# Shifting all SBUF tiles behind one small tile by 224 bytes in a Strassen QKV projection

## The chip, the cores and the metric

The kernel runs on one core of a Trainium2 chip. The metric is the device time of one execution in microseconds, as a median over executions; the span of a profile is about 2 us shorter than the time of the same execution. An execution counts as slow when it took over 1.5% more than the fastest of the same kernel, and as fast otherwise; of a program that ran once the state is unknown.

## The reference

```python
batch, seq, hidden = 16, 512, 768          # x: 16x512x768 float32, w_qkv: 768x2304 float32
qkv = np.matmul(x, w_qkv)
q, k, v = qkv[..., :hidden], qkv[..., hidden:2*hidden], qkv[..., 2*hidden:]
return np.stack([q, k, v], axis=0).astype(np.float32)
```

So it is one matrix product of 8192 rows by 768 by 2304, with the columns stored in three parts.

## The kernel before

The 2304 columns are two groups of 1024 (q=0 and q=1 in the code, called a and b here when they are used in a turn; a5 is product 5 of group a) and a remainder of 256. For each group and each 256 rows of x, a Strassen scheme makes the 2x2 block product from seven block products. Products 1 and 2 are in bf16, 3 to 7 in f32 (the type float32r). Each is three matmuls of 128x128 weights and 512 moving columns. A matmul has two operands: the weights, for which the trace shows a load of its own before each matmul, and the moving operand. The weights here are tiles of x (xb in bf16, or the sums s in f32), and the moving operands are tiles of w (b1 in bf16, t and b22 in f32).

```python
w_pool = ctx.enter_context(tc.tile_pool(name="w", bufs=1))
tq_pool = ctx.enter_context(tc.tile_pool(name="tq", bufs=2))
...                                   # bt, o, st, or, xin, xf pools
xb_pool = ctx.enter_context(tc.tile_pool(name="xb", bufs=4))
s_pool = ctx.enter_context(tc.tile_pool(name="s", bufs=2))
...
w_rem = w_pool.tile([P, KT, REM], bf16, name="w_rem")
b1 = [w_pool.tile([P, KT, CB], bf16, name=f"b1_{q}") for q in range(2)]
b22 = [w_pool.tile([P, KH, CB], f32r, name=f"b22_{q}") for q in range(2)]   # of both groups, product 3
t_0 = w_pool.tile([P, 4, KH, CB], f32r, name="t_0")          # moving tiles of group a
...
zero = w_pool.tile([P, CB], bf16, name="zero")
tiny = w_pool.tile([P, 1], fp32, name="tiny")                # takes 32 bytes
eye = w_pool.tile([P, P], bf16, name="eye")                  # 256 bytes, last tile of the pool w
...
t_1 = [tq_pool.tile([P, 2, KH, CB], f32r, name=f"t_1{n}", tag="tq") for n in range(2)]  # of group b
```

The next cut is condensed.

```python
def product(u, n, ps, start):
    t1, t2, t3, t4 = ts[u.q]
    if n <= 2:
        lhs, rhs = ...                # bf16: xb and b1
    else:
        k, t = {3: (4, b22[u.q][:]), 4: (0, t4), 5: (1, t1), 6: (2, t2), 7: (3, t3)}[n]
        lhs = [sr[u.p][:, k, j, :] for j in range(KH)]       # from an s tile
        rhs = [t[:, j, :] for j in range(KH)]
    for j in range(KH):
        nc.tensor.matmul(ps[:], lhs[j], rhs[j], ...)

def two(a, b, early):                 # one turn: 256 rows, both groups
    do(a, 1); do(b, 1); early()
    do(a, 2); do(a, 6); do(b, 2); do(b, 6)
    do(a, 5); do(a, 7); do(b, 5); do(b, 7)
    do(a, 4); rem(a.p); do(b, 4)      # rem: 12 bf16 matmuls of 256 columns
    do(a, 3); store_quad(a); do(b, 3); store_quad(b)
```

Pools lie one behind the other in SBUF. tiny and eye are the only tiles here whose size per partition is not a multiple of 512 bytes. So the size of eye, the last tile of w, decides at which byte, modulo 512, everything behind it starts.

Of the kernel before, what the change touches and what calls it, by code (L numbers as in the profile page):

```python
# [10 lines left out]
def kernel(  # L11
# [20 lines left out]
    nc = tc.nc  # L32
    P = 128
# [15 lines left out]
    bf16 = mybir.dt.bfloat16  # L49
# [9 lines left out]
    w_pool = ctx.enter_context(tc.tile_pool(name="w", bufs=1))  # L59
# [77 lines left out]
    def copy_halves(dst, src, two):  # L137

        nc.vector.tensor_copy(out=dst[0], in_=src[0])  # L139
        if two:  # L140
            nc.scalar.activation(dst[1], src[1], ident)  # L141
        else:
            nc.vector.tensor_copy(out=dst[1], in_=src[1])
# [10 lines left out]
    def turn_rows(p, two=True):  # L154
        c = xc.pop(p)
        xb[p] = xb_pool.tile([P, KT, 2 * P], bf16, name="xb")
        for r in range(2):
            cols = c[:, r, :].rearrange("m (p j) -> m j p", j=KT)
            ps = ps_pool.tile([P, KT, P], bf16, name="ps")
            for j in range(KT):  # L160
                nc.tensor.transpose(ps[:, j, :], cols[:, j, :], eye[:])  # L161
            ks = (slice(0, KH), slice(KH, KT))
            copy_halves(
                [xb[p][:, n, r * P:(r + 1) * P] for n in ks], [ps[:, n, :] for n in ks], two
            )
# [175 lines left out]
    load_rows(0)  # L341
    tiny = w_pool.tile([P, 1], fp32, name="tiny")
    nc.scalar.activation(tiny[:], zero[:, :1], ident)
    eye = w_pool.tile([P, P], bf16, name="eye")
    make_identity(nc, eye)
    load_rows(1)
    load_blocks(0, 0, 1)
# [64 lines left out]
    busy(11)  # L412
    cast_rows(0)
    turn_rows(0)
    busy(4)
    cast_rows(1)
    cast_k(0)
    cast_k(1)
    turn_rows(1)
    for j in range(2, KT):  # L420
        cast_k(j)
# [7 lines left out]
    rem(1)  # L429
    cast_rows(2, False)  # L430
    turn_rows(2, False)
    block(0, 0, b1[0], halves((4, 5)), nothing)
    for h in range(2):
# [63 lines left out]
```

## Time and profile before

| | before |
|---|---|
| median time | 367.14 us (366.95 to 367.59, 3 runs) |
| span of the profile | 364.8 us |
| TensorE busy | 358.0 us, 98% |
| granted TensorE clock, mean | 0.997 |
| period of one turn (42 matmuls of 512 columns, 12 of 256) | 10.873 us |

To read it: PE stands for TensorE's matmuls, PEld for its weight loads, DVE for VectorE, ACT for ScalarE, POOL for GpSimd. In a group row the number after x is the count, then come busy time in us, mean duration of one in ns, and the idle time of the engine just before. Matmul durations overlap, so a duration of 390 ns does not mean that one matmul takes 390 ns of the engine. What counts is the distance from one start to the next. Each position within a turn has nearly always the same distance (mostly within 2 ns), so a mean over turns resolves tenths of a nanosecond. The lines are in the prediction.

### The profile page before, as it was taken

What the parts mean: (1) busy time and instruction counts of PE and PEld (TensorE: products, weight loads), DVE (VectorE), ACT (ScalarE), POOL (GpSimd) and SP (SyncE); (2) the same over time, 40 slices, a digit from 0 to 9 for tenths busy, and PEclk for the clock granted to TensorE, in tenths of its full rate; (3) what the DMA queues carried; (4) which work ended last, traced back from release to release, by engine and by line L of the source; (5) the groups of instructions that cost most, each with busy time, mean ns of one, the idle gap of its engine ahead of it and who ended that gap; (6) DMA issues with size and microseconds to landing.
All of it is one profiled execution on the core that took longest, in us unless ns stands there. A gap on an engine that the chain in (4) does not pass through costs nothing.

```text
span 364.8 us, 5274 instructions
## 1 busy us (share of the span) xinstructions
PE 358.0 (98%) x1797; PEld 243.8 (67%) x1797; DVE 225.8 (62%) x239; ACT 182.4 (50%) x304; POOL 173.7 (48%) x180
## 2 busy tenths in 40 slices
PE   7999999999999999999999999999999999999995
PEld 3544576666776666776666777676777676777663
DVE  3589746765557665557666556666556766556732
ACT  4557554454454454554455544545545444445442
POOL 0000961655665445665444665444665544566410
PEclk9999999999999999999999999999999999999998
DMA  7999979988899899999888899888899989899767
GB/s 297 382 375 336 347 245 335 327 284 293 273 313 311 264 285 296 277 301 321 278 274 289 281 300 318 284 271 284 288 297 310 296 258 292 291 286 316 261 251 267
DMA packets 80617, 108.08 MB, mean 296 GB/s; under 512 B 4816, under 2 KB 60368, under 8 KB 80592
## 3 DMA queue, kind: packets, MB, share of 16 engines
q1 hardware_dynamic: 65184, 96.35, 80.8%
q10 hardware_dynamic: 15408, 11.41, 9.9%
q8 instruction: 14, 0.23, 0.3%
q14 instruction: 11, 0.09, 0.1%
HBM read 32.24 MB, written 75.50 MB: 295 GB/s over the span
## 4 chain that ended last, share of the span: by engine, by line
PE 97%; DMA 1%; ACT 1%; DVE 0%; issue 0%
PE ps L206 76%; PE ps L256 12%; PE ps L381 9%; DMA xin<-in_x_dram 1%; PE ps L161 1%; ACT xc L141 0%; ACT xb L141 0%; DVE xb L139 0%; ACT orem L311 0%
## 5 line engine op out<-in xcount | busy, mean ns | idle before, releaser
L206 PE MATMUL ps<-t,s 128*128 128x512 f32 x696 | 188.0, 412 | 0.0
L206 PEld LDWEIGHTS ps<-t,s 128*128 128x128 f32 x696 | 128.7, 188 | 30.9
L169 POOL CAST xb<-xf 128x1536 bf16<-128x1536 f32 x29 | 43.9, 1514 | 171.6 <-DVE xf L124 160.1
L124 DVE STREAM_TRANSPOSE xf<-xin 128x1536 f32<-128x1536 f32 x29 | 86.8, 2991 | 6.8 <-DMA xin<-in_x_dram 3.9
L206 PE MATMUL ps<-b,xb 128*128 128x512 bf16 x348 | 85.2, 381 | 0.0
L240 DVE TENSOR_TENSOR o<-o,ps 128x512 f32<-128x512 f32 x58 | 39.9, 688 | 59.3 <-PE ps L206 59.2
L234 DVE TENSOR_TENSOR o<-o,ps 128x512 f32<-128x512 f32 x58 | 39.8, 687 | 54.1 <-ACT o L233 54.1
L206 PEld LDWEIGHTS <-xb 128*128 128x128 bf16 x348 | 29.4, 98 | 42.8 <-issue 14.7
L233 ACT ACTIVATE o<-ps 128x512 f32<-128x512 f32 x58 | 34.8, 600 | 45.2 <-PE ps L206 45.2
L220 ACT ACTIVATE o<-ps 128x512 f32<-128x512 f32 x58 | 34.7, 599 | 43.3 <-DVE o L240 34.6
L227 ACT ACTIVATE o<-ps 128x512 f32<-128x512 f32 x58 | 34.8, 600 | 41.9 <-PE ps L206 41.9
L256 PE MATMUL ps<-w_rem,xb 128*128 128x256 bf16 x384 | 47.5, 273 | 0.0
L206 PE MATMUL ps<-b,s 128*128 128x512 f32 x174 | 44.9, 393 | 0.0
L256 PEld LDWEIGHTS <-xb 128*128 128x128 bf16 x384 | 35.0, 98 | 12.4 <-issue 8.1
L224 DVE TENSOR_TENSOR o<-o,ps 128x512 f32<-128x512 f32 x58 | 36.5, 669 | 2.3 <-ACT o L220 1.3
L206 PEld LDWEIGHTS ps<-b,s 128*128 128x128 f32 x174 | 32.7, 188 | 7.7
L237 ACT ACTIVATE o<-ps 128x512 f32<-128x512 f32 x58 | 34.7, 598 | 4.5 <-ACT orem L311 0.4
L178 POOL TENSOR_TENSOR s<-s,xf 128x384 fp32r<-128x384 f32 x29 | 30.1, 1038 | 2.3
L177 POOL TENSOR_TENSOR s<-xf 128x384 fp32r<-128x384 f32 x29 | 30.9, 1066 | 0.0
L266 ACT ACTIVATE orem<-ps 128x512 f32<-128x512 f32 x31 | 18.6, 599 | 23.5 <-PE ps L256 23.5
L181 POOL TENSOR_TENSOR s<-xf,s 128x384 fp32r<-128x384 f32 x29 | 29.5, 1019 | 0.0
L179 POOL TENSOR_TENSOR s<-xf 128x384 fp32r<-128x384 f32 x29 | 29.2, 1006 | 0.0
(36 smaller groups left out, 128.1 us busy)
## 6 DMA issues: line engine op xcount, KB each, us to landing
out_dram<-o SPq DMA_DIRECT2D x62, 768.0 KB, 5.2
out_dram<-o SPq DMA_DIRECT2D x65, 256.0 KB, 4.8
xin<-in_x_dram SPq DMA_DIRECT2D x62, 192.0 KB, 6.8
xin<-in_x_dram ACTq DMA_DIRECT2D x54, 192.0 KB, 5.6
out_dram<-orem SPq DMA_DIRECT2D x31, 256.0 KB, 2.3
st<-in_w_qkv_dram SPq DMA_DIRECT2D x6, 768.0 KB, 14.1
xin<-in_x_dram SPq DMA_DIRECT2D x3, 768.0 KB, 5.8
st<-in_w_qkv_dram SPq DMA_DIRECT2D x6, 256.0 KB, 6.2
```

The costliest lines, as they stand in the source:

```text
L124: nc.vector.transpose(t[:].rearrange("p j (g b) -> p g j b", b=G), xin.pop(p)[:].rearrange("p g (a j) -> p g j a", a=G),)
L169: nc.gpsimd.tensor_copy(out=xb[p][:], in_=xf[p][:])
L206: nc.tensor.matmul(ps[:], lhs[j], rhs[j], start=(start and j == 0), stop=(j == KH - 1), skip_group_check=True,)
L220: nc.scalar.activation(c11, u.x[:], ident)
L224: nc.vector.tensor_tensor(c11, c11, u.z[:], op=add)
L227: nc.scalar.activation(c12, u.x[:], ident)
L233: nc.scalar.activation(c22, u.x[:], ident)
L234: nc.vector.tensor_tensor(c22, c22, u.y[:], op=add)
L237: nc.scalar.activation(c21, u.x[:], ident)
L240: nc.vector.tensor_tensor(c12, c12, u.y[:], op=add)
L256: nc.tensor.matmul(ps, xb[p][:, j, r * P:(r + 1) * P], w_rem[:, j, :], start=(j == 0), stop=(j == KT - 1), skip_group_check=True,)
L381: nc.tensor.matmul(ps[n][:], xb[p][:, j, r * P:(r + 1) * P], w[:, j, :], start=(j == 0), stop=(j == KT - 1), skip_group_check=True,)
```

## The change

The intent is to have all operands of all products start at one offset modulo 512 bytes. eye keeps its 128 columns, but its tile is 240 columns wide, so 480 bytes are taken in place of 256.

```diff
-                nc.tensor.transpose(ps[:, j, :], cols[:, j, :], eye[:])
+                nc.tensor.transpose(ps[:, j, :], cols[:, j, :], eye)
...
-    eye = w_pool.tile([P, P], bf16, name="eye")
+
+    eye = w_pool.tile([P, 240], bf16, name="eye")[:, :P]
```

By the addresses that the allocator gives, w_rem, b1, b22 and t_0 lie at 128 modulo 512 in both kernels; t_1, xb, s and the rest lie at 416 before and at 128 after. b22 of both groups lies in w, so product 3 of b, too, had its operands at different offsets before.

## The prediction

> **What bounds the kernel now.** I read the page first: the busy row, the chain that ended last and the costliest groups. Then the chain in order of time, then short windows of the timeline, and last the start times of the individual matmul records of the trace.
>
> ```profile
> PE 358.0 (98%) x1797; PEld 243.8 (67%) x1797; DVE 225.8 (62%) x239; ACT 182.4 (50%) x304; POOL 173.7 (48%) x180
> ...
> PE 97%; DMA 1%; ACT 1%; DVE 0%; issue 0%
> ...
> L206 PE MATMUL ps<-t,s 128*128 128x512 f32 x696 | 188.0, 412 | 0.0
> L206 PEld LDWEIGHTS ps<-t,s 128*128 128x128 f32 x696 | 128.7, 188 | 30.9
> ...
> L206 PE MATMUL ps<-b,xb 128*128 128x512 bf16 x348 | 85.2, 381 | 0.0
> L206 PEld LDWEIGHTS <-xb 128*128 128x128 bf16 x348 | 29.4, 98 | 42.8 <-issue 14.7
> ...
> L206 PE MATMUL ps<-b,s 128*128 128x512 f32 x174 | 44.9, 393 | 0.0
> ```
>
> TensorE carries 97% of the chain, and its matmuls have 0.0 us of idle before them. No other engine is above 62%. So only the rate at which TensorE takes its matmuls sets the time, and a wait anywhere else is slack. The chain in order of time shows how regular this is:
>
> ```profile
> 161.10 1.33 PE ps L256 x12
> 162.43 9.55 PE ps L206 x42
> 171.97 1.33 PE ps L256 x12
> ```
>
> One turn of the loop (256 rows of x, both column groups) is 12 short and 42 long matmuls. Its period, from the start records, is 10.873 us, the same within 8 ns in all turns. There are 29 turns (the last in another order), so 315 of the 365 us are such turns.
>
> The matmul durations of the page overlap, so I used the distance from one start to the next. Means over 28 turns, in ns, the three matmuls of a product in order; a and b are column groups q=0 and q=1, the number is the Strassen product:
>
> a6 419, 229, 238; b6 417, 229, 233 (the first of each includes what the record before it gave up: 28+419 is 216+231); a5 234, 230, 235; a7 231, 229, 235; b5 231, 226.65, 226.65; b7 226.65 three times; a4 234, 235, 232; b4 314, 231, 236; a3 235, 231, 231; b3 229, 235, 232. Every bf16 product stands at 215.8, the 256-column ones at 109.
>
> So matmuls of one shape and type differ by up to 9 ns, each position always alike. Two windows of the timeline, a5 with a7 and then most of b5 with b7, show it without the records:
>
> ```profile
> 157.49 1.56 PE L206 MATMUL ps<-t,s 128*128 128x512 f32 x6
> ...
> 159.11 1.30 PE L206 MATMUL ps<-t,s 128*128 128x512 f32 x5
> ```
>
> Six overlapping records last five distances and one duration (394 ns in that window): (1.56-0.394)/5 = 233 ns. Five last four distances and one of 389 ns: (1.30-0.389)/4 = 228 ns. Same clock (1.00 in this stretch).
>
> What differs is the place of the operands. From the pool sizes of the kernel before, the pool w ends 288 bytes (tiny padded to 32, eye 256) past a multiple of 512 from its start. Thus w_rem, b1, b22, t_0 share one offset modulo 512 (128 by the allocator's addresses), and tq (t_1), xb, s and all later tiles share another (416). Each block of s, t, b1 and xb used here is a multiple of 512 or half of it. While an f32 matmul of a streams t_0 or b22 (128), the weights of the next are loaded from s (416); while one of b5 or b7 streams t_1 (416), weights come from s (416). Only this latter case reaches 226.65.
>
> **What the Trainium skill says.** (1) "TensorE: Matmul & The Clock Gate", section "Back-to-back issue gap": N/2.4 + 2.5 ns, thus 215.8 for 512 columns and 109.2 for 256. The trace agrees to 0.1 ns for bf16. So bf16 products have nothing to gain. (2) The same page, "Weight-path perf modes": fast weight load is on for 128 weights unless the type is FP32. The trace agrees in kind: loads of 98 ns in bf16, 188 in f32. In the fastest f32 stream a load starts 3 ns after the matmul before it, lasts 187.7, and the next matmul starts 35.6 ns after its end: 226.3. I take this as the floor for f32: weight loads, not columns. (3) "SBUF — State Buffer", "Who interferes with whom": TensorE has two independent read ports, one for the moving operand, one for weights, and PE never waits on anyone. The trace does not sit well with this: in the slow positions the lag from load end to matmul start is 40 to 45 ns instead of 35.6, though nothing but the operands' places differs. Neither page mentions a period of 512 bytes. (4) "DMA: Bandwidth & Descriptors", "How a descriptor splits into AXI transactions": starts at multiples of 256 B cost least. After the change the tiles lie at 128 modulo 256, before at 160, so neither has that; no run here shows an effect.
>
> **The change part by part.** It adds no instruction and removes none. eye takes 480 bytes in place of 256, so everything behind the pool w moves up by 224: 416 becomes 640, which is 128 modulo 512. All operands of all products then have one offset. The total grows by 224 bytes per partition and still fits. The identity keeps its place and is read by 36 transposes in the first 18 us only.
>
> What each position gains, taking b5/b7 as the model of an aligned stream (226.65), one settling step of 231 where a run of f32 has just begun (as b5 shows on its first), and nothing at positions where q=1 was aligned already:
> - a6: the first 419 to 417 as in b6 (2.5), the last before bf16 238 to 232 as in a4 and b3 (6.4): 9
> - a5: 3 + 3.3 + 8.4 = 15; a7: 4.2 + 2.5 + 8.4 = 15; b5: 4
> - a4: 7.6 + 8.4 = 16, its last (before bf16) stays
> - a3: 4 + 4.2 + 4.2 = 12; b3: 2.5 + 8.4 = 11, its last stays
> - b6, b7, b4: 0
>
> Sum 82 ns per turn, all on the path since TensorE has no idle. Times 29 turns: 2.4 us. The bf16 start (to 43.6 us, 216 ns per matmul) and the tail of 4.4 us stay. 367.14 - 2.4 = 364.7 us, a change of -0.65%.
>
> The uncertain step is settling. b6 and b4 are aligned now and yet run at 229, 233 and 231, 236: right after a switch from bf16, alignment did not help within three matmuls. If in the new kernel those also settle at once, the gain rises by about 31 ns (b6 9, b4 13, a5 and a3 4 each) to 113 ns: 3.3 us, 363.8. If the stream takes several more matmuls to settle after each switch, perhaps half the gain remains: 1.2 us, 365.9.
>
> **The rivals.** First: not equality but the absolute place of the moving operand counts (416 good, 128 bad). The evidence for it is equally b5 and b7, for they are the only t_1 streams long enough. Then b5 and b7 fall to the level of a5 and a7 (695 in place of 684 and 680, some 26 to 30 ns per turn): +0.9 us, 368.0. Against it: a mechanism of two reads meeting depends on their difference, and b6/b4, also at 416, are not fast. I give it one in six. Second: the two offsets do not matter, and phase alone (how far the load lags after a switch) makes the pattern; then nothing moves, 367.1. One in eight. Against it: b7 to a4 goes from 226.65 to 234 at the very change of moving operand, with no switch between. Third: the gain uncovers another bound. TensorE would need 0.8% less per turn, while from 43.6 to 356.8 us DVE is busy 194 of 313 us, ACT 155, POOL 165, and the DMA share is 0.90 at 291 GB/s (358 in the stretch before, so it can go higher). None becomes the bound. Fourth: DMA gains from the new places. In the steady turns it is hidden; only the first load (4.3 us of the chain) and the last stores could show, a tenth of a microsecond or two at most.
>
> **Range and chances.** Most of the weight lies between 363.8 and 365.9 around 364.7, with a quarter to a third for the first two rivals at 367 to 368. The range 363.4 to 366.9 should hold it 8 times in 10. To be faster by over 2% (under 359.8) a turn would have to lose 253 ns, but with every f32 matmul at the load floor of 226.65 it loses at most about 130. Slower by over 2% would need 250 ns more per turn, where the worst position now is 11 ns above the floor. So within 2% is nearly sure.
>
> **What would show it right or wrong.** Right: the pieces of 42 matmuls in the chain fall from 9.55 to about 9.47 us while those of 12 stay at 1.33; the x6 window of a5 and a7 falls from 1.56 to about 1.52; the group t,s falls from a mean of 412 to about 409.5, b,s from 393 to about 389; bf16 groups stay at 381 and weight loads at 188. The first rival: the windows of a and b become alike at the slower level. The second: the positions keep their numbers. Wrong in size: the positions right after a bf16 product show how long settling takes. The prediction fails outright if TensorE gets idle time, or if bf16 distances leave 216.

## The result

The changed kernel takes 365.01 us (364.97 to 365.77, 6 runs) against 367.04 us (366.92 to 367.59, 6 runs). The ratio is 0.9946, with a 95% interval of 0.9933 to 0.9958. A ratio here is the mean time of one kernel's fast runs over that of the other's in the same rounds, so it is not quite the ratio of the medians quoted. A change clear of noise, and within the 2% that count as the same.

The page of the changed kernel, in the same parts as before (busy row, groups):

```profile
PE 354.3 (98%) x1765; PEld 244.0 (67%) x1797; DVE 224.2 (62%) x239; ACT 182.2 (50%) x304; POOL 173.8 (48%) x180
...
L206 PE MATMUL ps<-t,s 128*128 128x512 f32 x696 | 186.5, 410 | 0.0
L206 PEld LDWEIGHTS ps<-t,s 128*128 128x128 f32 x696 | 128.8, 188 | 29.7
...
L206 PE MATMUL ps<-b,s 128*128 128x512 f32 x174 | 44.5, 391 | 0.0
```

The reader should see three things. The f32 matmuls are 2 ns shorter on the mean (412 to 410 and 393 to 391). The weight loads have their old 188 ns. And this trace holds 1765 matmuls for 1797 weight loads: 32 matmul records are missing, so its busy time is not to be compared (all 696 + 174 f32 matmuls are there). The same kernel was therefore profiled again (the run after_again below), and that trace is complete. Its chain in order of time (start in us, length in us, what), around one turn:

```profile
160.62 1.33 PE ps L256 x12
161.94 9.48 PE ps L206 x42
```

The 12 short matmuls are as before, and the 42 long ones went from 9.55 to 9.48 us. Its timeline in the two windows that the prediction used, a5 with a7 and then most of b5 with b7:

```profile
157.05 1.52 PE L206 MATMUL ps<-t,s 128*128 128x512 f32 x6
...
158.64 1.30 PE L206 MATMUL ps<-t,s 128*128 128x512 f32 x5
```

The window of group a fell from 1.56 to 1.52 us, and that of b stayed at 1.30. With a duration of 389 ns in the first window the distance is (1.52-0.389)/5 = 226 ns: group a has come to the level of b. The period of a turn fell from 10.873 to 10.807 us in both traces of the changed kernel. That is 66 ns, and over 29 turns 1.9 of the 2.0 us between the medians.

### The profile page after: what moved, and what is told of

It is laid out like the page before. It is cut to its first block, busy times and chain, and to the rows that moved or that the text cites. A ratio compares the mean times of both kernels' runs of the same rounds, so it can differ in the third digit from the quotient of the medians.

```text
span 362.8 us, 5242 instructions
## 1 busy us (share of the span) xinstructions
PE 354.3 (98%) x1765; PEld 244.0 (67%) x1797; DVE 224.2 (62%) x239; ACT 182.2 (50%) x304; POOL 173.8 (48%) x180
## 4 chain that ended last, share of the span: by engine, by line
PE 96%; ACT 1%; issue 1%; ACTq 0%; DVE 0%
PE ps L206 75%; PE ps L256 11%; PE ps L382 9%; PE ps L362 1%; PE ps L161 0%; ACT o L237 0%; ACTq L297 0%; ACT xb L141 0%; ACT orem L311 0%; DVE xb L139 0%; ACT xc L141 0%; ACTq L313 0%; DVE zero L340 0%; ACTq L311 0%
## 5 line engine op out<-in xcount | busy, mean ns | idle before, releaser
L169 POOL CAST xb<-xf 128x1536 bf16<-128x1536 f32 x29 | 46.4, 1600 | 169.5 <-DVE xf L124 167.5
L206 PE MATMUL ps<-b,xb 128*128 128x512 bf16 x320 | 79.0, 380 | 1.9
L233 ACT ACTIVATE o<-ps 128x512 f32<-128x512 f32 x58 | 34.7, 598 | 44.1 <-PE ps L206 44.1
L177 POOL TENSOR_TENSOR s<-xf 128x384 fp32r<-128x384 f32 x29 | 29.3, 1010 | 0.0
L179 POOL TENSOR_TENSOR s<-xf 128x384 fp32r<-128x384 f32 x29 | 29.1, 1002 | 0.0
```

The costliest lines, as they stand in the source:

```text
L169: nc.gpsimd.tensor_copy(out=xb[p][:], in_=xf[p][:])
L206: nc.tensor.matmul(ps[:], lhs[j], rhs[j], start=(start and j == 0), stop=(j == KH - 1), skip_group_check=True,)
L233: nc.scalar.activation(c22, u.x[:], ident)
```

## The experiments

The twelve runs were made in three sets; each set was timed beside the kernel before on one chip. "Difference" means the start of s less the start of the moving tile. In the kernel before it is 288 for group a and 0 for b, in the changed kernel 0 for both. Product 3 of b goes with group a in this, since its moving tile b22 lies beside t_0. The diffs are against the changed kernel unless they say otherwise. A padding tile that is never used costs no instruction.

### all_416: all operands together at another place

```diff
+    lead = w_pool.tile([P, 144], bf16, name="lead")      # 288 bytes, ahead of w_rem
     w_rem = w_pool.tile([P, KT, REM], bf16, name="w_rem")
```

> The changed kernel with 288 unused bytes ahead of all tiles: all operands at 416 modulo 512 in place of 128. Theory (equality): pattern and time of the changed kernel, settled f32 matmuls at 226.65, a turn of 10.807 us, 365.0 us, ratio about 0.9946. Rival (s at 128 is what is good, 416 is bad for it): a5, a7, a4 and b5, b7 slow, 230 to 235, time of the kernel before or 1 us above.

Measured: 365.66 us (365.0 to 365.75), ratio 0.9957 (0.9943 to 0.9972), turn 10.807 us. Every position of a turn has the distance it has in the changed kernel, within 0.5 ns. Its chain around one turn has the pieces of the changed kernel:

```profile
160.96 1.33 PE ps L257 x12
162.28 9.48 PE ps L207 x42
```

So the place itself does not count, neither that of s nor that of the moving tile. The executions fall on two levels, 365.0 and about 365.7; in the profiled one (365.62) the first long matmuls of the turns stand in the chain at 45.48 us, in the changed kernel's (364.97) at 44.84, so what differs lies ahead of the turns. The changed kernel too had one execution at 365.77, so the new place is not needed for it; why it came oftener here (three of four) is open.

### half: a difference of 256 for group a

```diff
-    eye = w_pool.tile([P, 240], bf16, name="eye")[:, :P]
+    eye = w_pool.tile([P, 368], bf16, name="eye")[:, :P]
```

> Padding of eye such that s and t_1 lie at 384 and t_0, b22 at 128: difference 256 in column group 0, 0 in group 1. Theory (period of 512): group 0 stays slow, b5 and b7 stay at 226.65, time within 1 us of the kernel before (366 to 368). Rival (the period is 256 or a divisor of it): group 0 as fast as in the changed kernel, ratio 0.9946.

Measured: 365.67 us (365.03 to 365.79), ratio 0.9958 (0.9943 to 0.9973), turn 10.807 us. Its timeline in the window of a5 with a7:

```profile
156.82 1.52 PE L206 MATMUL ps<-t,s 128*128 128x512 f32 x6
```

It reads as in the changed kernel, though s lies 256 bytes off t_0. My expectation was wrong and its rival right: the rule needs no 512, and 256 (or a divisor of it) is enough.

### near: differences of 32 bytes

```diff
+    gap_pool = ctx.enter_context(tc.tile_pool(name="gap", bufs=1))   # between xb and s
     s_pool = ctx.enter_context(tc.tile_pool(name="s", bufs=2))
...
+    gap = gap_pool.tile([P, 16], bf16, name="gap")
...
-    eye = w_pool.tile([P, 240], bf16, name="eye")[:, :P]
+    eye = w_pool.tile([P, 208], bf16, name="eye")[:, :P]
```

> s lies 32 bytes behind t_1 (difference +32, group 1) and 32 bytes ahead of t_0 and b22 (difference -32, group 0), modulo 512. Theory as told (exact equality): both groups slow, 229 to 236, turn of 10.88 us or more, ratio 1.000 to 1.004. Rival (only a coarse distance counts, 32 bytes are next to nothing): both fast, ratio 0.9946. If one sign is fast and the other slow, the order of the two reads counts and not equality.

Measured: 369.11 us (369.02 to 369.39), ratio 1.0058 (1.0041 to 1.0074), turn 10.940 us. Its timeline in the windows of a5 with a7 and of b5 with b7:

```profile
158.37 1.56 PE L208 MATMUL ps<-t,s 128*128 128x512 f32 x6
...
160.00 1.33 PE L208 MATMUL ps<-t,s 128*128 128x512 f32 x5
```

Now b is slow as well: (1.33-0.396)/4 = 234 ns with the 396 ns of that window. So 32 bytes, ahead or behind, are enough to lose the pace. (With a period of 256, the 288 of the kernel before are 32 as well.) The turn is 67 ns above the kernel before (a slow, b fast) and 133 ns above the changed kernel (both fast). Of the 67 ns, 47 stand in b6, b5, b7 and b4, which lost their equal offset; the other 20 stand in products that had unequal offsets in both kernels (a6 and b3 above all), so it seems to count somewhat in which way two operands are apart. The kernel before thus had a third to a half of what equal offsets are worth without the change.

### mid: differences of 128 and 64 bytes

```diff
+    gap = gap_pool.tile([P, 32], bf16, name="gap")       # 64 bytes, between xb and s
...
-    eye = w_pool.tile([P, 240], bf16, name="eye")[:, :P]
+    eye = w_pool.tile([P, 272], bf16, name="eye")[:, :P]
```

> s stands 128 bytes past t_0 and b22 (group 0) and 64 bytes past t_1 (group 1). The run half showed 256 to be as good as 0. If the period is 256: both groups slow, 229 to 236, turn about 10.94 us as in near, some 369 us. If it is 128: group 0 fast, group 1 slow. If it is 64 (near excludes 32): both fast, 365.0 us.

Measured: 368.43 us in its one execution (state unknown, granted clock 0.997), turn 10.927 us. Its timeline in the windows of a5 with a7 and of b5 with b7:

```profile
158.00 1.55 PE L208 MATMUL ps<-t,s 128*128 128x512 f32 x6
...
159.62 1.33 PE L208 MATMUL ps<-t,s 128*128 128x512 f32 x5
```

In group a (difference 128) a5 and a7 have distances of 228 to 233 ns, in b (64) b5 and b7 have 231 to 239. Neither reaches 226.65. A period of 128, or of any divisor of it, would have made 128 as good as 0. So the period is 256.

### s16: 16 and 48 bytes

```diff
-        s = s_pool.tile([P, 5, KH, P], f32r, name="s")
+        s = s_pool.tile([P, 5 * KH * P + 8], f32r, name="s")
+        s = s[:, 4:4 + 5 * KH * P].rearrange("p (a j m) -> p a j m", a=5, j=KH)
```

> The changed kernel with the contents of s moved by 16 bytes within tiles that are 32 bytes longer, so that s stands 16 bytes past t_0, t_1 and b22 in every second turn and 48 bytes past them in the others. Theory (only equality modulo 256 counts): no position settles at 226.65, both kinds of turn take 10.92 to 10.95 us, 368.5 to 369.2 us. Rival (16 bytes fall into one and the same line or block and are as good as 0): turns alternate between about 10.81 and 10.94 us, some 367 us.

Measured: 368.56 us in its one execution (state unknown, granted clock 1.0). The turns alternate between 10.932 and 10.935 us, so 16 bytes are as bad as 48. The distances in b7 are 234, 233, 234 and 233, 233, 233 ns. Its timeline in the window of b5 with b7:

```profile
159.64 1.33 PE L207 MATMUL ps<-t,s 128*128 128x512 f32 x5
```

This run is the cleanest of all: every other tile lies where it lies in the changed kernel, and only the start of s differs. So it is the place of s against the moving tile that costs, and not that of another tile which the padding shifts along. Of all differences tried (0, 16, 32, 48, 64, 128, 224, 256, 288) only 0 and 256 gave a stream at 226.65.

### s_only, s_only2, s_only3: group a aligned in place of b

```diff
+    gap = gap_pool.tile([P, 112], bf16, name="gap")      # 224 bytes, between xb and s
...
-    eye = w_pool.tile([P, 240], bf16, name="eye")[:, :P]
+    eye = w_pool.tile([P, 128], bf16, name="eye")[:, :P]
```

Now t_0, b22 and s share 128 modulo 512, and t_1 stays at 416: difference 0 for a, 224 for b. Against the kernel before, s alone has moved.

> Only the s tiles (weights of the f32 products) move by 224 bytes: t_0, b22 and s now share 128 modulo 512, while t_1 stays at 416. Theory (only equality of the moving and the weight offset counts): the fast and the slow side change places. Products a5, a7, a4, b3 run at 226.65 ns per matmul, b5 and b7 at 229 to 235; a turn loses about 69 ns and gains about 26, some -43 ns net, 365.8 us, ratio about 0.9966. Rival (the weights' own place counts, s at 128 is good): a and b both at 226.65, ratio 0.9946 as in the changed kernel. Rival (the moving operand's own place counts): pattern and time of the kernel before, ratio 1.000.

Measured: 367.9 us as the median of four, one of which is the profiled execution at 744.35; the three fast ones are at 367.68 to 368.03, ratio 1.002 (1.0004 to 1.0037). So it is slower than the kernel before, where I had expected 0.9966. The profile fell in a slow execution and cannot say why, as this row of its groups shows:

```profile
L208 PE MATMUL ps<-t,s 128*128 128x512 f32 x696 | 369.7, 707 | 0.0
```

Every matmul took about twice as long there.

> The same program as s_only, whose profiled execution ran all matmuls at about 443 ns and shows nothing of the offsets. Timed before: ratio 1.002, where the theory had given 0.9966. Theory, mended: equal offsets (t_0, b22, s at 128) bring nothing in the first two or three f32 matmuls after each change between group 0 and group 1 or bf16, so only the second half of a5 with a7, and b3, reach 226.65, and b5, b7, b4 (difference 224) run at 229 to 236. Then the period should be about 10.90 us. Rival (the weights' own place is what counts): no long runs at 226.65 in group 0 at all.

Measured: 367.79 us, ratio 1.0019 (1.0003 to 1.0034) from three fast runs, and the profiled execution was slow again (523.36 us, granted clock 0.656). So the time stood, and the trace was of no use.

> s_only for the third time, now last of its set: the two looks before came in executions whose matmuls ran at a half or two thirds of the clock. Theory (equality, with settling after each change of distance): group 0 reaches 226.65 within a7, a4 or b3 but not at once, b5 and b7 (distance 224) run at 229 to 236, turn about 10.90 us. Rival (the weights' own place): group 0 never at 226.65.

Measured: 367.7 us in its one execution (state unknown, granted clock 0.997), turn 10.900 us. Its timeline in the windows of a5 with a7 and of b5 with b7:

```profile
157.76 1.55 PE L208 MATMUL ps<-t,s 128*128 128x512 f32 x6
...
159.38 1.33 PE L208 MATMUL ps<-t,s 128*128 128x512 f32 x5
```

Group b lost its stream: (1.33-0.395)/4 = 234 ns with the 395 ns of that window. Group a gained, but late: the distances of a5 and a7 are 230, 236, 228, 233, 231 and 226.5 ns, those of a3 and b3 230, 232.5, 231, 227, 227 and 230 (the last stands before bf16). So b5 and b7 at a weight place of 128 are slow, which settles that the place of s alone is not what counts. And equality needs time to work. Five matmuls of a5 and a7 pass before 226.5 is reached, and a4, after b7, reaches it nowhere (230, 236, 232), though its difference is 0 too. As it seems, group a comes in runs that are too short, and each change between the groups starts again; so the sides could not simply change places, as I had first expected. Why a run settles sooner or later is not shown.

### after_again: the changed kernel, repeated

> The changed kernel once more, beside the runs below. Both theories: ratio 0.9946, 365.0 us or, as all_416 and half showed in some executions, 365.7; settled f32 matmuls at 226.65 ns, turn of 10.81 us.

Measured: 365.08 us (364.97 to 365.49), ratio 0.9947 (0.9935 to 0.996), turn 10.807 us. This is the complete trace used above. The distances per product, as sums of the three matmuls in ns, means over 28 turns (a6, b6 and b4 begin with a record that includes what the one before it gave up):

| product | before | predicted change | changed kernel | change | near | s_only3 |
|---|---|---|---|---|---|---|
| a6 | 886 | -9 | 885 | -1 | 893 | 892 |
| b6 | 879 | 0 | 882 | +3 | 885 | 884 |
| a5 | 699 | -15 | 681 | -18 | 700 | 694 |
| a7 | 695 | -15 | 680 | -15 | 698 | 690 |
| b5 | 684 | -4 | 680 | -4 | 700 | 703 |
| b7 | 680 | 0 | 680 | 0 | 702 | 700 |
| a4 | 701 | -16 | 683 | -18 | 696 | 698 |
| b4 | 781 | 0 | 785 | +4 | 785 | 786 |
| a3 | 697 | -12 | 692 | -5 | 699 | 693 |
| b3 | 696 | -11 | 683 | -13 | 706 | 684 |

The bf16 matmuls stand at 215.6 to 216.0 in all of these (apart from the one right after f32), whatever the difference between xb and b1. So the runs with a single execution, s_only3 here and also mid and s16 (215 to 216), did not run at a slower clock.

### one_switch and one_switch_before: fewer changes between bf16 and f32

What the changed kernel still has above its floors sits beside the changes of type. So I put all bf16 matmuls of a turn ahead of all f32 ones:

```diff
         do(a, 2)
-        do(a, 6)
         do(b, 2)
+        rem(a.p)
+        do(a, 6)
         do(b, 6)
 ...
         do(a, 4)
-        rem(a.p)
         do(b, 4)
```

> The changed kernel with the products of a turn in another order: all bf16 products and the remainder first, then all f32 products, one switch from bf16 to f32 per turn in place of three. In the changed kernel a turn is 111 ns above the sum of its floors (12 of 215.85, 12 of 109.15, 30 of 226.65), nearly all of it beside the switches. Theory (settling belongs to the switch): two entries and two exits go, about 60 ns per turn, 1.7 us in 28 turns, 363.3 us, ratio about 0.990 to the kernel before. Rival (the first product into a bank now waits for an eviction, or the order costs elsewhere): same or slower than 365.0 us, with idle time on TensorE.

> The kernel before with the same new order. Theory: the entries and exits saved are worth about as much, some 30 to 60 ns per turn, 365.5 to 366.3 us, but a, with difference 288, stays at 229 to 236, so it stays 1.5 to 2.5 us above one_switch. Rival (the gain of the change was only in settling after switches): both orders equal once there is one switch, within 0.5 us of one_switch.

Measured: one_switch 372.29 us, ratio 1.015 (1.0136 to 1.0164), turn 11.067 us; the same order in the kernel before 374.43 us, ratio 1.0201 (1.0187 to 1.0215), turn 11.153 us. Both are slower, and the waits of one_switch (who waited for whom, us in total, times, longest) say why:

```profile
PEld ps L206 <- ACT o L233: 12.1, 28, 0.4
```

L233 is ScalarE's copy of block c22 out of the bank (of PSUM, where TensorE's sums are kept) into which product 4 of b adds next. The remainder between a4 and b4 had been hiding that copy. Without it the weight load of b4 waits once per turn, 0.4 us each. A part of this is covered by the matmul still running: the turn is 0.31 us longer than in one_switch_a3 below, which has as few changes of type and no such wait. This was the rival that I had named. What the pair still tells is that the padding is worth 86 ns per turn in this order too, 2.1 us between the medians. So the gain is not in settling alone. (The first of the two expectations puts a turn of the changed kernel 111 ns above the sum of its floors. The floors that it names add up to 10.700 us, so it is 107.)

### one_switch_a3: the same, with product 3 of a in the gap

```diff
         do(a, 4)
-        rem(a.p)
-        do(b, 4)
         do(a, 3)
         store_quad(a)
+        do(b, 4)
         do(b, 3)
```

(with the bf16 part as in one_switch)

> The changed kernel with one switch per turn, as in one_switch, but product 3 of a stands between product 4 of a and product 4 of b, so that b4 need not wait for the ScalarE copy out of its bank (in one_switch TensorE waited 12.1 us for it over 28 turns). Theory (the loss of one_switch was that wait alone, and switches cost settling): the wait goes, a turn of 10.75 to 10.78 us in place of 10.81, 363.5 to 364.2 us, ratio about 0.991. Rival (what one_switch lost was more than the wait): 366 us or above.

Measured: 363.27 us (363.23 to 363.6), ratio 0.9898 (0.9883 to 0.9913), against 0.9947 for the changed kernel in the same rounds. The chain in order of time:

```profile
155.12 1.31 PE ps L256 x12
156.44 9.45 PE ps L206 x42
```

The wait is gone, and a turn takes 10.760 us in place of 10.807. From a7's second matmul to b3's second the f32 matmuls run at 226 to 227 without a break. The ten before it, from a6 on, lie between 224 and 236, so settling took longer than the two or three matmuls I had counted on. This version beats both kernels. It is correct by comparison with the reference.

## Why the prediction was right

The time was predicted as 364.7 us in a range of 363.4 to 366.9 and is 365.01; the gain was put at 2.4 us and is 2.0.

- **TensorE sets the time, so the gain is read from its distances.** Right. Idle before the f32 matmuls stayed at 0.0 us, and 66 ns per turn times 29 turns is 1.9 us of the 2.0.
- **f32 matmuls have a floor of 226.65 ns when both operands are aligned.** Right. All matmuls of a5, a7, b5 and b7 and the first two of a4 have it within 0.4 ns in the changed kernel, and no run went more than 0.4 ns below it in a settled stream. That the weight load is what sets it (188 ns in the f32 groups, 189 and 190 in s16) is consistent with the trace, but no run varied the load's length by intent, so this stays argued.
- **Equality, not place.** Right, and shown: all_416 keeps the gain at another place, s_only3 shows weights at 128 that are slow with a moving tile at 416, and t_0 became fast without moving.
- **bf16 has nothing to gain.** Right: 215.8 before and after. (The section that the prediction cites calls its formula that of an isolated matmul, and gives about 131 ns for a sustained stream of 512 columns; in this kernel's streams it was 215.8, so the formula fits here and that figure does not.)
- **Settling after a switch is unchanged at b6 and b4, one step at a5 and a3, and the last of a6 drops by 6.** This was the mis-sized term. a6's last matmul did not drop (238 to 239), which with the first costs 8 of the 9 ns put there. a3 gave 5 in place of 12, because b4 ends unsettled and two of a3's matmuls still run at 232.5 and 231. b6 and b4 became 3 and 4 ns slower. On the other side a5, a4 and b3 gave 2 to 3 ns more each. Together the turn gained 66 ns and not 82, so the errors cancel in part: about 22 ns too little in some places, about 7 more in others.
- **Rivals.** No other engine became a bound. DMA shows no gain in the turns, which TensorE sets. The rivals of place and of phase alone fell as told above. What decides how many matmuls pass before an aligned stream settles is not known.
- **Two figures.** The prediction says that a turn could lose at most about 130 ns with every f32 matmul at 226.65. Its own distances give 142; neither is near the 253 ns that 2% would have needed. And its lag of 40 to 45 ns from load end to matmul start in the slow positions is 37 to 45 in the records.
- **The 512 in the prediction.** I took the modulus from the change and reasoned with it. The run half shows that 256 does as well.

What stays open is the mechanism: why two reads that start at equal bytes modulo 256 get along, while those 16 bytes apart cost about 7 ns per matmul, and why settling takes three matmuls in one place and ten in another. That the two reads from SBUF are what meets is a guess; the runs show only that the two start addresses do it together.

## What to carry to other kernels

In a TensorE-bound f32 kernel, try weight tiles and moving tiles at equal addresses modulo 256 bytes (shown here for float32r with 128x128 weights, new for each matmul, and 512 columns), and do it for all of them: s_only aligned one group in place of the other and lost. Compare start-to-start distances position by position: matmuls of one shape that differ by a few nanoseconds, always at the same positions, are a sign of it. Keep matmuls of one type in long runs, but look for the bank copies that the interruptions were hiding before reordering. A small tile at the end of a pool moves all pools behind it, so a gain or a loss of half a per cent can come from a tile that has nothing to do with it.

## What the Trainium skill lacked or had wrong

- "TensorE: Matmul & The Clock Gate", "Step-by-step: what each phase is for", says: "Loading the next tile's weights doesn't steal SBUF read bandwidth from the running matmul." "SBUF — State Buffer", "Who interferes with whom", says that PE never waits on anyone. Here f32 matmuls ran at 226.65 ns with a difference of 0 or 256 bytes between the start of weights and moving operand, and mostly at 228 to 236 with the other differences tried. In a whole kernel that was 365.01 against 369.11 us (the run near). Neither page mentions a period of 256 bytes. That it is the two reads which disturb each other is not shown.
- The same TensorE page, "LDWEIGHTS (loading the stationary operand)", gives P/1.2, thus 107 ns for 128 columns. The loads here took 98 ns in bf16 and 188 ns in f32. It gives no distance for f32 matmuls, which here was 226.65 ns at best with new weights each time, against 215.8 in bf16.
- No page tells what a change between bf16 and f32 costs. Here the first bf16 matmul after f32 took 11 ns more than those behind it, and the f32 stream with equal offsets needed three to ten matmuls to reach its pace.
- "Perfetto Trace Analysis" does not warn that a trace may lack single matmul records: 32 of 1797 were missing in one profile of the changed kernel and none in the other (32 also in s_only2, mid, one_switch and one_switch_before).
- "TensorE: Matmul & The Clock Gate", "Seeing it yourself", warns that clock events can be unreliable and that the clock was seen stuck low for over 50 us. Here two whole executions of the program s_only were slow, 744 and 523 us in place of 368, the first with most bf16 matmuls at 443 ns in place of 216. The recorded mean clock was 1.0 in the first, which does not fit its pace, and 0.656 in the second. The same program ran normally in six timed executions beside them; the cause is not known.
